# Early projection blocks of a hybrid decoder layer in 1024-column blocks, three of eight steps by seven products

## The chip, the cores and the metric

One core of one Trainium2 chip runs the whole layer in one launch. The metric is the device time of that core in microseconds, the median of several runs.

## The reference

One layer on 256 positions of width 2048 (float32):

```python
a = rmsnorm(h, norm_mix_pre)
proj = a @ w_in                       # 2048 x 17408
q_a, k_a, v_a, q_r, f_r, i_r, g_r, gate_a, gate_r = split_columns(proj)
# attention: 3 groups (window, dilation) x 8 heads of 128, rotary q and k,
#            group outputs mixed by their softmax denominators
# recurrence: S_t = diag(f_t) S_{t-1} + k_t v_t^T, o_t = S_t^T q_t, 8 heads,
#            f = lb + (1 - lb) sigmoid(f_r), k = 1 - f, per-head RMSNorm, gain, times silu(g_r)
y = sigmoid(gate_a) * (attn @ w_attn_branch) + sigmoid(gate_r) * (r_out @ w_hgrn_branch)
h = h + rmsnorm(y @ w_mix_out, norm_mix_post)
a = rmsnorm(h, norm_ffn_pre)
gt, up = split(a @ w_ffn_gate_up)     # 2048 x 11264
h = h + rmsnorm((silu(gt) * up) @ w_ffn_down, norm_ffn_post)
```

The columns of `w_in` are q, k, v (3072 each), the recurrence's q, f, i, g (1024 each) and the two gates (2048 each).

## The kernel before

Every product is made of three matmuls in a rounded format: the kernel splits each float32 operand into a high and a low part, ScalarE writing the high one (a copy), VectorE the low one (a subtraction), and adds high x high, high x low and low x high in PSUM. The weights stream once from memory, through three slots of 8 KB per partition (`raw`), and are split into `w` slots two steps ahead of TensorE (`AHEAD`).

The work is a list of blocks, written out in program order. Each engine takes its instructions in the order in which the Python loop issues them.

- An "N" block makes 512 columns with the activations as the stationary operand: 8 chunks of 12 matmuls. The value blocks take every second position of `xT` for a side (`parity`), for the attention's dilation. A "W" block makes 256 columns with the weights as the stationary operand (4 chunks of 16 matmuls), so that its result comes out transposed.
- A wide block (`Wide`) makes 1024 columns in steps of 256 rows of weights. A whole step has 24 matmuls. A step "by seven" takes seven products of three matmuls for eight, by sums of weight blocks (VectorE, `split_wide`) and of activation blocks (`seven_sums`). Four of the products (p1, p5, p6, p7) have PSUM banks of their own, which `gather` adds up after the last step by seven; the four results, keys (side, group), are added to that by the evacuation. A wide block thus holds all eight banks, and the next one uses the two groups of four (`acc`, `aux`) the other way round. The high and low parts of the raw differences (`dh`, `dl`) have one buffer each.

In the loop over wide steps, step i comes in this order: the split of step i + 2, the loads, the matmuls of step i (`multiply_wide`), `gather` after the last step by seven, one turn of the evacuation that stands first in `evacs`; in the feed-forward also, at step 1, `turn_act`, which transposes on TensorE the product u of gate and up of the block before. At the end of a block its evacuation joins `evacs` and takes its first turn.

Program order before: g (2 N blocks), f and the recurrence's q (W), i (N), then twice, once for each half of the heads, three value blocks (N) and six rotary q and k blocks (W); eight gate blocks (N); eight branch blocks, attention and recurrence in turn; the mix (N); then the feed-forward: a first gate and a first up block (N), ten wide gate/up blocks (`GATE_UP`: eight steps, of which the third, fifth and seventh by seven), and two wide down blocks (`DOWN`: 22 steps, six by seven, with `prep`, which makes the activations' sums).

Beside the blocks run two `lanes` of generators, one turn of each per chunk: the opening (norm, tables), the recurrence of each half (its levels, with work on GpSimd, ScalarE, VectorE and small matmuls), and the attention of each head (15 turns). `flush(lanes...)` before the branch blocks ends what is left of them. Large intermediate tiles (`fslot`) share 15 slots.

Of the kernel before, what the change touches and what calls it, by code (L numbers as in the profile page):

```python
# [2 lines left out]

# [16 lines left out]
P = 128  # L20
# [16 lines left out]
H7 = (0, 1, 2)  # L37
GATE_UP = [(3, 0), (4, 0), (0, 1), (5, 0), (1, 1), (6, 0), (2, 1), (7, 0)]
DOWN = [[(m, m in by7) for m in range(KF // 2)] for by7 in (range(4, 20, 3), range(3, 19, 3))]

N_RAW, N_SPLIT, AHEAD, WARM, BRIDGE = 6, 3, 2, 8, 6


class Block:
# [7 lines left out]
    def __init__(self, kind, w, nk, col, xs, evac, parity=False, pre=None, mid=None, post=None):  # L52
        self.kind, self.w, self.nk, self.col = kind, w, nk, col
        self.xs, self.evac, self.parity = xs, evac, parity
        self.pre, self.mid, self.post = pre, mid, post
        self.per = 4 if kind == "W" else 2
        self.width = 1024 // self.per
        self.steps = nk // self.per
        self.banks = None


class Wide:
# [7 lines left out]
    def __init__(self, w, cols, order, xs, seven, evac, prep=None, pre=None, turn=1):  # L70
        self.w, self.cols, self.order, self.xs, self.seven = w, cols, order, xs, seven
        self.evac, self.prep, self.pre, self.turn = evac, prep, pre, turn
        self.last7 = max(i for i, (m, s) in enumerate(order) if s)
        self.bank, self.open, self.rest = {}, set(), None
# [3 lines left out]
def tile_hybrid_block(ctx: ExitStack, tc: tile.TileContext, t, out):  # L78
# [29 lines left out]
    def p3(s, dtype, n, bufs, tag=None):  # L108
        return act_pool[0].tile([P, n], dtype, tag=tag or s, bufs=bufs, name=nm(s))
# [34 lines left out]
    eps = cpool.tile([P, 2], F32, name="eps")  # L144
# [7 lines left out]
    r1p = cpool.tile([P, 2], F32, name="r1p")  # L152
# [4 lines left out]

    ph1 = ExitStack()
    kp = ph1.enter_context(tc.tile_pool(name="kp", bufs=1, reuse_waits="tile"))
    fp = ph1.enter_context(tc.tile_pool(name="fp", bufs=1, reuse_waits="tile"))  # L160

    act_pool = []

    def fslot(s):
        return fp.tile([P, 1024], F32, tag="f", bufs=15, name=nm(s))

    def ptile(s):
        pool, n = (act_pool[0], 2) if act_pool else (fp, 5)
        return pool.tile([P, 512], F32, tag="p", bufs=n, name=nm(s))

    cs = kp.tile([P, 2, S], F32, name="cs")
# [5 lines left out]
    gainr = kp.tile([P, HW], F32, name="gainr")  # L177
    tabs = kp.tile([P, 4, S], F32, name="tabs")
    lb = kp.tile([P, 8], F32, name="lb")
    lb1 = kp.tile([P, 8], F32, name="lb1")  # L180


    blocks, chunks, pairs = [], [], []
    wides, steps = [], []

    def add(*args, **kw):
        b = Block(*args, **kw)
        blocks.append(b)
        for c in range(b.steps):
            chunks.append([b, c, None, None, None])  # L190

    def add_wide(w, nk, col, xs, ev):
        for i in range(2):
            add("W", w, nk, col + 256 * i, xs, both_halves(ev, i))
# [11 lines left out]
    def parts(j):  # L206

        return (slice(0, 512), slice(512, 1024)) if j == 0 else (slice(0, 1024),)

    def load(j):  # L210
        if j >= len(chunks):
            load_wide(j - len(chunks))
            return
        b, c = chunks[j][:2]
        if j % 2 == 0:
            pairs.append(stream.tile([P, 2048], F32, tag="raw", bufs=N_RAW // 2, name=nm("raw")))
        raw = pairs[j // 2][:, j % 2 * 1024 : j % 2 * 1024 + 1024]
        rows = b.per * P
        src = b.w[c * rows : (c + 1) * rows, b.col : b.col + b.width]
        src = src.rearrange("(k p) c -> p k c", p=P)  # L220
        dst = raw.rearrange("p (k c) -> p k c", k=b.per)
        n = len(parts(j))
        for i in range(n):
            ks = slice(i * b.per // n, (i + 1) * b.per // n)
            nc.sync.dma_start(dst[:, ks, :], src[:, ks, :])
        chunks[j][2] = raw
# [4 lines left out]
    def split(j, only=None):  # L231
        if j >= len(chunks):
            split_wide(j - len(chunks))
            return
        raw = chunks[j][2]
        if chunks[j][3] is None:
            w = wslot()
            chunks[j][3:] = [w[:, :1024], w[:, 1024:]]
        wh, wl = chunks[j][3:]
        for n, k in enumerate(parts(j)):  # L240
            if only in (None, n):
                nc.scalar.activation(wh[:, k], raw[:, k], AF.Copy)  # L242
                nc.vector.tensor_sub(wl[:, k], raw[:, k], wh[:, k].bitcast(F32))  # L243

    def multiply(j, sides=(0, 1)):
# [4 lines left out]
        for s in sides:  # L250
            if s == 1 and c == 0 and b.mid:
                b.mid()
            for kk in range(b.per):
# [3 lines left out]
                if b.kind == "N":  # L257
                    ps = b.banks[s]
                    if b.parity:
                        sh, sl = (  # L260
                            x.rearrange("p (j two) -> p two j", two=2)[:, s, :]
                            for x in (xh, xl)
                        )
                    else:
                        sh, sl = (x[:, s * P : (s + 1) * P] for x in (xh, xl))
# [9 lines left out]
    def add_wide_block(*args, **kw):  # L275
        b = Wide(*args, **kw)
        wides.append(b)
        for i in range(len(b.order)):
            steps.append([b, i, None, None])

    def load_wide(n):
        if n % 2 or n // 2 >= len(steps):
            return
        n //= 2
        b, i = steps[n][:2]
        m = b.order[i][0]
        raw = stream.tile([P, 2048], F32, tag="raw", bufs=N_RAW // 2, name=nm("raw"))
        for g, col in enumerate(b.cols):
# [1151 lines left out]
```

## Time and profile before

| | us |
|---|---|
| median of 3 runs | 1741.58 (1741.17 to 1743.07) |
| span of the profiled execution | 1740.1 |
| PE busy | 1725.0 |
| DVE busy | 1264.3 |
| ACT busy | 886.1 |
| POOL busy | 74.0 |

The profiled execution's span is 1.48 us below the median of the runs. A busy PE is the time in which at least one matmul is on record; matmuls overlap in the array, so that the pitch from one to the next is read from the start times, not from the duration of one. L115 is the helper through which nearly all matmuls go; the tile names tell them apart. L243 and L242 are the split of chunks, L306 and L308 that of whole wide steps, L312 to L326 that of steps by seven, L371 to L375 `gather`, L1161 to L1167 the feed-forward's evacuation, L1127 `turn_act`.

### The profile page before, as it was taken

To read this page: it belongs to the slowest core of one execution; us is meant where nothing else is said; L and a number is where in the kernel's file an instruction comes from. 1 tells how busy PE (TensorE), PEld (TensorE's weight loads), DVE (VectorE), ACT (ScalarE), POOL (GpSimd) and SP (SyncE) were. 2 spreads that over 40 slices of the span, in tenths; PEclk is the share of its full clock that TensorE was granted. 3 is DMA by queue.
4 is the path that set the end of the run, shared out by engine and by line. 5 is a ranking of instruction groups with operands and counts; after the bars stand their busy time and mean duration, and the time that the engine had idled before them with its cause. 6 is when DMAs were issued, how large, how long until landed. Compare 5 with 4: busy or idle time off the path is not lost.

```text
span 1740.1 us, 21588 instructions
## 1 busy us (share of the span) xinstructions
PE 1725.0 (99%) x8424; PEld 1448.6 (83%) x8424; DVE 1264.3 (73%) x1372; ACT 886.1 (51%) x1050; POOL 74.0 (4%) x54
## 2 busy tenths in 40 slices
PE   9999999999999999999999999999999999999997
PEld 7888888888888888888888877888888888888886
DVE  5767647877546776544566577888888888898998
ACT  6545455344444444454444466555555555665663
POOL 0002413400000000000000000000000000000000
PEclk9999999999999999999999999999999999999999
DMA  7655445455454554455555745655555555666553
GB/s 271 202 192 194 145 150 165 146 160 186 163 170 161 185 188 169 170 169 193 193 179 185 266 168 175 214 199 201 205 194 194 194 194 199 221 209 218 195 197 116
DMA packets 201222, 325.91 MB, mean 187 GB/s; under 512 B 10096, under 2 KB 76832, under 8 KB 201120
## 3 DMA queue, kind: packets, MB, share of 16 engines
q1 hardware_dynamic: 198848, 319.41, 54.4%
q10 hardware_dynamic: 2272, 5.12, 0.8%
q8 instruction: 66, 1.08, 0.2%
q14 instruction: 36, 0.29, 0.1%
HBM read 322.40 MB, written 2.10 MB: 186 GB/s over the span
## 4 chain that ended last, share of the span: by engine, by line
PE 95%; DVE 2%; ACT 1%; issue 1%; DMA 0%; POOL 0%; DVEq 0%; ACTq 0%
PE acc L115 71%; PE aux L115 22%; DVE w L243 1%; ACT w L242 1%; DVE w L677 0%; PE aux L453 0%; PE aux L724 0%; DMA gpost<-in_norm_mix_post 0%; PE acc L1127 0%; DVE fz L1256 0%; PE aux L1127 0%; DVE x L776 0%; PE aux L440 0%; ACT junk L1210 0%; POOL x L770 0%
## 5 line engine op out<-in xcount | busy, mean ns | idle before, releaser
L243 DVE TENSOR_TENSOR w<-raw,w 128x1024 fp32r<-128x1024 f32 (+1 forms) x353 | 444.4, 1260 | 365.5 <-ACT w L242 362.7
L242 ACT ACTIVATE w<-raw 128x1024 fp32r<-128x1024 f32 (+1 forms) x353 | 372.9, 1057 | 481.1 <-PE acc L115 470.7
L115 PE MATMUL acc<-w,xT 128*128 128x512 f32 x1728 | 409.1, 395 | 0.0
L115 PEld LDWEIGHTS acc<-w,xT 128*128 128x128 f32 x1728 | 326.3, 191 | 65.8
L115 PE MATMUL acc<-xT,w 128*128 128x256 f32 (+1 forms) x2048 | 362.6, 338 | 0.0
L115 PEld LDWEIGHTS acc<-xT,w 128*128 128x128 f32 x2048 | 313.0, 189 | 45.1
L308 DVE TENSOR_TENSOR wl<-raw,w 128x2048 fp32r<-128x2048 f32 x82 | 187.5, 2287 | 34.0 <-ACT w L306 33.9
L306 ACT ACTIVATE w<-raw 128x2048 fp32r<-128x2048 f32 x82 | 156.6, 1910 | 81.7 <-PE aux L115 32.1
L115 PE MATMUL acc<-w,hT 128*128 128x512 f32 x622 | 182.5, 392 | 1.5 <-DVE w L243 1.2
L115 PEld LDWEIGHTS acc<-w,hT 128*128 128x128 f32 x622 | 115.8, 188 | 26.9 <-DVE w L243 2.5
L115 PE MATMUL aux<-w,hT 128*128 128x512 f32 x430 | 135.7, 389 | 0.0
L324 DVE TENSOR_TENSOR wl<-sum,w 128x2048 fp32r<-128x2048 f32 x42 | 96.2, 2290 | 33.8 <-ACT w L320 32.7
L317 ACT ACTIVATE w<-sum 128x1024 fp32r<-128x1024 f32 x42 | 44.7, 1063 | 111.0 <-DVE sum L312 106.7
L115 PEld LDWEIGHTS aux<-w,hT 128*128 128x128 f32 x430 | 80.7, 188 | 16.7
L115 PE MATMUL acc<-w,yT 128*128 128x512 f32 x384 | 88.0, 390 | 0.3 <-DVE w L243 0.3
L115 PEld LDWEIGHTS acc<-w,yT 128*128 128x128 f32 x384 | 71.8, 188 | 15.5 <-DVE w L243 0.7
L115 PE MATMUL acc<-w,a 128*128 128x512 f32 x268 | 83.7, 389 | 0.0
L115 PE MATMUL aux<-w,a 128*128 128x512 f32 x268 | 83.7, 389 | 0.0
L115 PE MATMUL aux<-wl,hT 128*128 128x512 f32 x215 | 83.7, 389 | 0.0
L115 PE MATMUL acc<-wl,hT 128*128 128x512 f32 x215 | 83.7, 389 | 0.0
L326 DVE TENSOR_TENSOR dl<-raw,dh 128x1536 fp32r<-128x1536 f32 x42 | 73.5, 1751 | 0.0
L323 ACT ACTIVATE dh<-raw 128x1536 fp32r<-128x1536 f32 x42 | 61.9, 1474 | 0.0
(263 smaller groups left out, 2015.3 us busy)
## 6 DMA issues: line engine op xcount, KB each, us to landing
raw<-in_w_in SPq DMA_DIRECT2D x271, 512.0 KB, 4.5
raw<-in_w_ffn_gate_up SPq DMA_DIRECT2D x176, 512.0 KB, 4.4
raw<-in_w_ffn_down SPq DMA_DIRECT2D x88, 512.0 KB, 4.8
raw<-in_w_mix_out SPq DMA_DIRECT2D x32, 512.0 KB, 4.9
raw<-in_w_attn_branch SPq DMA_DIRECT2D x16, 512.0 KB, 4.5
raw<-in_w_hgrn_branch SPq DMA_DIRECT2D x16, 512.0 KB, 4.6
hx<-in_x ACTq DMA_DIRECT2D x4, 512.0 KB, 9.9
x<-in_x SPq DMA_DIRECT2D x3, 512.0 KB, 10.0
```

What stands on the lines that cost most here:

```text
L115: nc.tensor.matmul(ps, lhsT, rhs, start=start, stop=stop, skip_group_check=True)
L242: nc.scalar.activation(wh[:, k], raw[:, k], AF.Copy)
L243: nc.vector.tensor_sub(wl[:, k], raw[:, k], wh[:, k].bitcast(F32))
L306: nc.scalar.activation(hi, raw, AF.Copy)
L308: nc.vector.tensor_sub(lo, raw, hi.bitcast(F32))
L317: nc.scalar.activation(hi[:, :1024], s[:, :1024], AF.Copy)
L323: nc.scalar.activation(dhi, d, AF.Copy)
L324: nc.vector.tensor_sub(lo, s, hi.bitcast(F32))
L326: nc.vector.tensor_sub(dlo, d, dhi.bitcast(F32))
```

## The change

- The gates of the attention branch, half of those of the recurrence branch, the values, g and i become eight wide blocks of 1024 columns (`early`) at the start of the kernel. The first (`PLAIN`) has no steps by seven, the other seven have `GATE_UP`. The sums of `xT` (`pair_sums`) are made during the first. The remaining two gate blocks stay N blocks, behind the q and k blocks.
- Gates and values are put in DRAM (`stored`, issued from ScalarE's queue, one store per 128 x 512 tile) and fetched (SyncE's queue) before they are used: the values at the last k block of each half, the gates behind all q and k blocks. The values are fetched with the rows' parity apart, so the strided weights of the value blocks go.
- In a step by seven of a block without `prep`, the products from the sums (`by_sums`) go before those from the raw differences (`by_raw`, of which p1 is the last). That holds for the early blocks and for the feed-forward's ten gate/up blocks; the down blocks keep their order.
- Lanes advance twice in a wide step (`between`). A recurrence level has one turn more between its last elementwise product and its matmuls. The heads go into one `queue`, and a lane that is empty takes the next.
- All four recurrence-branch blocks go before the four attention-branch blocks. `turns` advance twice per chunk.
- `fslot` has 16 slots. The early blocks have a pool of their own (`p0`), closed during the first f block; two small tiles are padded, so that the pools behind them start at other addresses.

The core of the diff:

```diff
+    def totals(b, then):
+        while "r1c" not in ready:
+            yield
+        for n, key in enumerate(((0, 0), (0, 1), (1, 0), (1, 1))):
+            src = b.bank[key]
+            if b.rest:
+                nc.vector.tensor_add(b.rest[key], src, b.rest[key])
+                src = b.rest[key]
+            then(key, src)
+            if n % 2:
+                yield
+    def stored(names, func):
+        def ev(b):
+            def then(key, src):
+                s, g = key
+                e = b.rest[key] if b.rest else eslot()
+                nc.scalar.activation(e, src, func, scale=r1c[:, s : s + 1])
...
+                nc.scalar.dma_start(waits[names[g]][s * P : (s + 1) * P, :], e)
+            return totals(b, then)
+        return ev
+    def evac_g(b):
+        def then(key, src):
...
+            sig = ptile("sig")
+            nc.scalar.activation(sig, src, AF.Sigmoid, scale=r1c[:, s : s + 1])
+            nc.vector.scalar_tensor_tensor(
+                out=sig, in0=src, scalar=r1c[:, s : s + 1], in1=sig, op0=OP.mult, op1=OP.mult
+            )
+            nc.vector.tensor_mul(gN[g][:, s, :], sig, gainr[:, g * 512 : (g + 1) * 512])
+        return totals(b, then)
...
-        prod((0, 1), act_of(0, 1), d, 2)
-        prod((0, 0), sums(3), d, 0)
-        prod("p1", act_of(0, 0), d, 1, last)
-        prod("p6", sums(1), t, 2, last)
-        prod("p5", sums(0), t, 1, last)
-        prod("p7", sums(2), t, 0, last)
-        prod((1, 1), act_of(1, 1), t, 3)
+        def by_raw():
+            prod((0, 1), act_of(0, 1), d, 2)
+            prod((0, 0), sums(3), d, 0)
+            prod("p1", act_of(0, 0), d, 1, last)
+        def by_sums():
+            prod("p6", sums(1), t, 2, last)
+            prod("p5", sums(0), t, 1, last)
+            prod("p7", sums(2), t, 0, last)
+            prod((1, 1), act_of(1, 1), t, 3)
+        for part in (by_raw, by_sums) if b.prep else (by_sums, by_raw):
+            part()
+            if part is by_raw or not b.prep:
+                between()
+                between = lambda: None
...
             nc.gpsimd.tensor_mul(xv[:, :, right], xv[:, :, right], qv[:, :, right])
             yield
+            yield
             ps = aux()
...
+    early = [
+        (("a", 0), ("a", 1), COL_GA, 512),
+        (("a", 2), ("a", 3), COL_GA + 1024, 512),
+        (("r", 0), ("r", 1), COL_GB, 512),
+    ]
+    early += [(("v", g, 0), ("v", g, 1), COL_V + 1024 * g, 512) for g in range(3)]
+    early += [("g", "g", COL_GR, 512), ("i", "i", COL_IR, 512)]
+    for n, (k0, k1, col, step) in enumerate(early):
+        ev = {"i": evac_i, "g": evac_g}.get(k0) or stored(
+            (k0, k1), AF.Copy if k0[0] == "v" else AF.Sigmoid
+        )
+        add_wide_block(w_in, (col, col + step), GATE_UP if n else PLAIN, xT,
+                       lambda m: x7[m], ev, n % 2 == 0, mid=more_x if n == 0 else None, halves=n == 0)
```

More of the change, by code (lines that the diff above doesn't have):

```diff
@@ L204, in both_halves, with add_wide_block @@
         return go
[L206 to L212, printed above, removed]
-            return
[L214 to L226, printed above, removed]
+    def add_wide_block(*args, **kw):
+        b = Wide(*args, **kw)
+        wides.append(b)
+        for i in range(len(b.order)):
+            n = len(steps)
+            slots.append(lambda n=n: load_wide(n))
+            items.append((steps, n, len(slots) - 1))
+            steps.append([b, i, None, None])
@@ L501, in flush, with advance_lanes, flush_lanes @@
             advance(q)
+    def advance_lanes():
+        for lane in lanes:
+            if not lane and queue:
+                lane.append(queue.popleft())
+            advance(lane)
+    def flush_lanes():
+        while queue or any(lanes):
+            advance_lanes()
     xt = [hslot("x") for _ in range(4)]
@@ L653, in nslot, with fetch, fetch_values @@
     def nslot(s):
         return fslot(s).rearrange("p (b c) -> p b c", b=2)
[L656 to L662 removed]
+    def fetch(dst, key, rows, **sizes):
+        nc.sync.dma_start(dst, waits[key].rearrange(rows, **sizes))
+    def fetch_values(half):
+        for g in range(3):
+            vN[half, g] = nslot("v")
+            fetch(vN[half, g], ("v", g, half), "(j two) c -> j two c", two=2)
@@ L778, in level @@
             yield
+            yield
             ps = aux()
```

430 lines of the change are left out of this document (227 added, 203 removed).

## The prediction

> **What bounds the kernel now.** I read the page first, for the engine that fills the span; then the chain of waits, for what one matmul costs in each stage; then the timelines of one feed-forward block, engine by engine, for the spare time around the matmuls.
>
> ```profile
> span 1740.1 us, 21588 instructions
> ...
> PE 1725.0 (99%) x8424; PEld 1448.6 (83%) x8424; DVE 1264.3 (73%) x1372; ACT 886.1 (51%) x1050; POOL 74.0 (4%) x54
> ...
> PE 95%; DVE 2%; ACT 1%; issue 1%; DMA 0%; POOL 0%; DVEq 0%; ACTq 0%
> ...
> raw<-in_w_in SPq DMA_DIRECT2D x271, 512.0 KB, 4.5
> ```
>
> TensorE is never out of work and carries 95% of the chain. So the time changes by matmul time taken out, plus every new wait of TensorE.
>
> ```profile
> 497.01 11.20 PE acc L115 x48
> ...
> 661.78 10.93 PE acc L115 x48
> ...
> 1159.68 10.88 PE aux L115 x48
> ...
> 1202.05 10.88 PE acc L115 x48
> ...
> 1244.59 10.88 PE aux L115 x48
> ...
> 1286.96 10.88 PE acc L115 x48
> ...
> 1414.08 10.88 PE aux L115 x48
> ```
>
> The chain's columns are start, time, what. Durations of single matmuls overlap; the pitch is these times over 48: 233.3 ns in the value blocks (every second column of xT as weights), 227.7 ns in the gate blocks, 226.7 ns in the wide blocks. A whole step (24 matmuls) is 5.44 us, a step by seven (21) 4.76 us. The last five rows each open a feed-forward block at its step 0; I call that instant T.
>
> **What the change takes out.** Sixteen 512-column blocks (gates a, half of gates r, values, g, i) become eight wide ones, one whole and seven with three steps by seven: 16 x 96 = 1536 matmuls become 192 + 7 x 183 = 1473. 63 x 0.2267 = 14.3 us. The 576 matmuls of the values lose the strided weights: 576 x 6.6 ns = 3.8 us. The other 960 go from 227.7 to 226.7 ns: 1.0 us. Together **-19.1 us**, all on the path. Everything else of TensorE (f, qr, q, k, branches, mix, FFN) has as many matmuls as before.
>
> **What the new order inside a step by seven adds in the feed-forward.** Where a block has no `prep`, `by_sums` now goes before `by_raw`, so p1 is the last product of the step, not the third of seven. The ten gate/up blocks have no `prep` either. `gather` starts with p1.
>
> ```profile
> 1408.13 0.68 DVE L372 TENSOR_TENSOR e<-aux,e 128x512 f32<-128x512 f32 x1
> 1410.92 2.28 DVE L308 TENSOR_TENSOR wl<-raw,w 128x2048 fp32r<-128x2048 f32 x1
> 1413.12 2.48 DVE L1161 TENSOR_TENSOR e<-acc,e 128x512 f32<-128x512 f32 x4
> 1415.51 1.21 DVE L312 TENSOR_TENSOR sum<-raw 128x1024 f32<-128x1024 f32 x1
> 1416.76 0.69 DVE L318 TENSOR_TENSOR sum<-raw,sum 128x512 f32<-128x512 f32 x1
> ...
> 1419.30 2.29 DVE L324 TENSOR_TENSOR wl<-sum,w 128x2048 fp32r<-128x2048 f32 x1 [1.13 <-ACT w L320]
> 1421.51 1.75 DVE L326 TENSOR_TENSOR dl<-raw,dh 128x1536 fp32r<-128x1536 f32 x1
> 1423.18 1.41 DVE L1167 SCALAR_TENSOR_TENSOR e<-e,r2c,e 128x512 f32<-128x512 f32 x2
> ```
>
> ```profile
> 1405.96 0.60 ACT L371 ACTIVATE e<-aux 128x512 f32<-128x512 f32 x1
> 1408.68 1.92 ACT L306 ACTIVATE w<-raw 128x2048 fp32r<-128x2048 f32 x1 [2.12 <-PE acc L115]
> 1413.84 0.73 ACT L1164 ACTIVATE e<-e,r2c 128x512 f32<-128x512 f32 x1 [3.23 <-DVE e L1161]
> 1418.21 1.06 ACT L320 ACTIVATE w<-sum 128x1024 fp32r<-128x1024 f32 x1 [0.31 <-DVE sum L319]
> 1420.55 1.90 ACT L306 ACTIVATE w<-raw 128x2048 fp32r<-128x2048 f32 x1
> ```
>
> With T = 1414.08, step 6 ends at T-5.44. Before, p1 is copied (L371) at T-8.12 and the first add (L372) runs at T-5.95. With p1 last the copy starts at T-5.40 and ends at T-4.80: the add at T-4.75, 1.20 us later. From there DVE has no slack until L1167: split, four adds, sums, two lows, then the two multiplies that make u (the 1.13 us idle before L324 is ScalarE's answer to those same sums). So u comes 1.20 us later, and TensorE's next work after step 1 (T+10.88) is the transpose of u, in order.
>
> How much room is there? One block of the trace answers:
>
> ```profile
> 1203.83 1.22 DVE L312 TENSOR_TENSOR sum<-raw 128x1024 f32<-128x1024 f32 x1
> ```
>
> Here the sums start at T+1.78 (T = 1202.05), not T+1.43: 0.35 us late. From the chain, that block lasts 1244.59 - 1202.05 = 42.54, its neighbours 42.37 (1159.68 to 1202.05; 1244.59 to 1286.96). 0.35 us late cost 0.17, so the room is 0.18 us, and 1.20 us late costs 1.02. Nine blocks transpose a u made so: **+9.2 us**. Bounds: 0 (something absorbs it) and 9 x 1.2 = 10.8.
>
> **What the early blocks' evacuation adds.** They have the same step order, and the evacuation comes in two turns: keys (0,0), (0,1) at the block's end, (1,0), (1,1) after the next block's step 0, on DVE behind the split of step 2. New here: each key's tile is stored to DRAM from ScalarE's queue.
>
> ```profile
> 956.63 0.90 ACTq L985 DMA_DIRECT2D gpost<-in_norm_mix_post  x2
> 957.56 3.34 ACTq L991 DMA_DIRECT2D hx<-in_x  x4
> 960.95 0.60 ACT L1002 ACTIVATE junk<-acc 128x512 f32<-128x512 f32 x1 [3.26 <-issue]
> ```
>
> ```profile
> 1.23 0.93 SPq L225 DMA_DIRECT2D raw<-in_w_in  x2
> ```
>
> ScalarE waits while it issues. An issue took 0.45 (gpost), 0.47 (SP's 256 KB pieces, the shape of a store) or 0.84 us (hx). I take 0.47, and 0.1 for the store's wait on its own tile. On the clock of T: first add 0.24 (as above), sums at 1.5; ScalarE is held by two functions of 0.72 and two issues to 3.5; its halves to 5.6; lows 7.9 and 9.55; adds 10.2 and 10.8; function, store, function, store: 12.8. Only now comes step 3's split: ScalarE 14.7, DVE 17.0. TensorE is there at 10.88 + 4.76 = 15.64 and waits 1.4. Step 4's sums start at 17.0, its low ends 6.1 later (as L312 to the end of L324), TensorE is there at 22.45: 0.6 more. 2.0 us at each of the five ends of stored blocks with products by seven: **+10.0 us** (no issue cost: 0.3 each, 1.5; at 0.84: 3.5 each, 17.5). Block 0 has no adds and no gather: 0, covered by some 2 us of room.
>
> Block g is worse: add, sigmoid on ScalarE, multiply, multiply, in DVE's order, so DVE stands through each sigmoid.
>
> ```profile
> 58.81 0.69 ACT L644 ACTIVATE sig<-acc,r1c 128x512 f32<-128x512 f32 x1
> ```
>
> ```profile
> 61.62 0.75 DVE L646 SCALAR_TENSOR_TENSOR sig<-acc,r1c,sig 128x512 f32<-128x512 f32 x1
> 62.40 0.69 DVE L649 TENSOR_TENSOR g<-sig,gainr 128x512 f32<-128x512 f32 x1
> ```
>
> A key takes 2.85 us, a turn 5.7. Sums of step 2 at 5.95, low at 12.0 (TensorE there at 10.88: 1.1); second turn 13.6 to 19.3, its last sigmoid at 17.9, then step 3's split 19.8 and 22.05 (TensorE there at 16.8: 5.3); step 4 0.6. **+7.0 us**; bounds 1 (DVE catches up) and 9.
>
> **What moves.** Both recurrences now run under the q/k blocks with their rotary evacuation; before, the first ran under i and v.
>
> ```profile
> 145.00:277.00 132.00, 131.64 (x653) 111.41 (x652) 82.12 (x82) 65.99 (x94) 32.88 (x19) 0.99 0.47 160
> ...
> 285.00:332.00 47.00, 45.32 (x288) 40.26 (x287) 44.33 (x40) 19.65 (x28) 25.00 (x12) 0.96 0.42 135
> ```
>
> ```profile
> 304.64 1.97 PE L115 MATMUL aux<-x 128*128 128x64 f32 x16 [1.45 <-DVE x L776]
> ...
> 321.40 1.97 PE L115 MATMUL aux<-x 128*128 128x64 f32 x16 [0.23 <-DVE x L776]
> ...
> 332.41 11.41 PE L115 MATMUL acc<-xT,w 128*128 128x512 f32 x64
> ```
>
> ```profile
> 295.43 4.15 DVE L677 TENSOR_TENSOR w<-sum,tabs 64x512 f32<-64x512 f32 x2
> ...
> 329.86 1.38 DVE L677 TENSOR_TENSOR w<-sum,tabs 64x512 f32<-64x512 f32 x2
> ```
>
> Columns: span; busy of PE, PEld, DVE, ACT, POOL; granted clock; DMA. Under q/k, DVE is busy 44.33 of 47 us (L677 takes 4.15 us beside POOL, 1.38 without); TensorE loses 1.68 idle (1.45 + 0.23 for late x) and 4% of clock, 1.9: 3.6 us. Under i and v it loses 0.36 + 1% of 132: 1.7. Two under q/k, with the added turn covering the idle 1.68 of each: 3.8 against 5.3 now, **-1.5 us**. Bounds: no loss left (-5.3), and each losing double (+9.1).
>
> Costed at nothing: 24 stores and 12 fetches, beside a DMA share of 0.4 to 0.5; the fetches stand on SP ahead of weights, whose three slots hold six W chunks (2.85 us each, 11.41 for four) against 4.5 us to land, so a fetch that waits two chunks for its slot is covered. The second half's attention has 32 turns in two lanes under gate and recurrence-branch chunks (32); what is left, the last two splits, is wanted three chunks later. Startup loads the same bytes for its first product.
>
> Sum: -19.1 + 9.2 + 10.0 + 7.0 - 1.5 = **+5.6 us** on the span of 1740.1. The median of the runs is 1741.58, 1.48 above that span; I add the sum to it: 1747.
>
> **Rivals.** (1) Faster: the early blocks' waits are not there, since a store issue does not hold ScalarE and DVE catches up before step 3. For: DVE's work in such a block is 3 x 6.6 (1.21 + 2 x 0.69 + 2.29 + 1.75) + 5 x 2.29 + 8 adds of 0.62 = 36 of 41.5 us (183 x 0.2267). Against: L1002's 3.26. -19.1 - 1.5 + 9.2 = -11.4: 1730. It decides once the early waits sum to under 7.9 of the 17.0 (then faster by over 3.5). (2) Only the feed-forward wait is absorbed: 5.6 - 9.2 = -3.6: 1738. Against it stands the 42.54. (3) A store issue costs 0.84, as hx: +7.5: 1755. (4) DVE and POOL pace the q/k blocks at the upper bound: +10.6: 1758. (5) TensorE's 5.3 us stop after g lowers the clock: the 285 to 332 window shows 0.96 around a 1.45 us stop, 1.9 us; it would give 1749. The Trainium skill ("TensorE: Matmul & The Clock Gate", Part 1) puts half clock after an idle window of about 3.4 us; by it, an estimate, 1.7 us more.
>
> **How the numbers follow.** Forecast 0.42, (1) 0.25, (2) 0.12, (3) 0.09, (4) 0.06, (5) 0.06. A change of under 0.2% (3.5 us) can't be told from none: 1738.1 and 1745.1 are the borders. Faster: (1) and 0.08 of (2), 0.33. Same: the rest of (2) and 0.13 of the forecast's lower end, 0.17. Slower 0.50. The forecast's own range is 1741 to 1752; 8 in 10 needs (1) and (3): 1728 to 1756.
>
> **What would show it.** Before each transpose of u, TensorE idle about 1 us, released by DVE; feed-forward blocks of 43.4 us. In each early block after the second, a stop before step 3, the longest after g. Matmuls down by 63, value pitch at 226.7. Wrong if the gate/up blocks stay at 42.4, or early wide blocks last 41.5 us each.

## The result: 1763.5 us, slower

The changed kernel takes 1763.49 us (median; 1761.73 to 1764.46), 21.9 us more than the 1741.55 us of the kernel before beside it: ratio 1.0124, 95% interval 1.0110 to 1.0138. The direction was the forecast's, the size was not: 1763 lies above the range's upper end, 1756.

The page of the changed kernel, span, busy times and the chain's shares by engine:

```profile
span 1762.7 us, 21573 instructions
...
PE 1719.0 (98%) x8356; PEld 1432.1 (81%) x8357; DVE 1390.0 (79%) x1466; ACT 917.3 (52%) x1052; POOL 77.2 (4%) x54
...
PE 70%; DVE 16%; issue 6%; ACT 5%; DMA 2%; ACTq 0%; POOL 0%; SPq 0%; DVEq 0%; POOLq 0%
```

Line numbers are now the changed kernel's: L119 is the helper that was L115. TensorE's share of the chain falls from 95% to 70%, VectorE's rises from 2% to 16%. Outside its busy time TensorE spends 1762.7 - 1719.0 = 43.7 us instead of 15.1: 28.6 us more idle. Its busy time falls by 6.0 us, not by the 19.1 of the forecast; part of the difference is clock, as the next views show. TensorE's waits, by who ended them (us in total, times, longest):

```profile
PE acc L119 <- DVE w L295: 6.4, 6, 2.0
PE acc L119 <- ACT xT L524: 3.8, 1, 3.8
PE aux L119 <- DVE wl L342: 3.6, 3, 1.8
PE aux L1218 <- DVE e L1258: 2.7, 10, 0.3
PE acc L119 <- DVE wl L342: 2.5, 3, 1.0
...
PE aux L119 <- DVE x L884: 2.1, 2, 1.1
```

L295 is mostly the split of the q and k chunks, L524 the copies of the transposed input, L342 the low half of a whole wide step's split (L340 the high one), L1258 the feed-forward's u, L884 a recurrence level's product. Two of these stand nowhere in the forecast's sum: L295 and L524. (L358 and L360, in later views, are the low halves of a step by seven.) The table of stages shows the same (columns: span; busy of PE, PEld, DVE, ACT, POOL; granted clock; DMA), the start, the other early blocks, q and k with the recurrences; the last row is the start of the kernel before:

```profile
6.00:70.00 64.00, 58.33 (x258) 46.16 (x256) 44.93 (x76) 39.66 (x65) 0.00 (x0) 0.95 0.70 247
70.00:375.00 305.00, 293.89 (x1273) 238.64 (x1272) 248.54 (x200) 157.35 (x131) 0.95 (x1) 0.99 0.63 211
470.00:660.00 190.00, 182.58 (x1132) 160.44 (x1131) 173.69 (x182) 88.07 (x140) 65.88 (x33) 0.99 0.48 157
```

```profile
6.00:70.00 64.00, 63.77 (x316) 52.38 (x314) 44.08 (x68) 41.65 (x68) 0.00 (x0) 1.00 0.76 262
```

TensorE idles 5.7 us in the start, 11.1 in the early blocks and 7.4 under q and k. The start of the kernel before loses 0.2.

### The profile page after: what moved, and what is told of

Same layout as the page of the kernel before. It is cut to its first block, busy times and chain, and to the rows that moved or that the text cites. A ratio compares the mean times of both kernels' runs of the same rounds, so it can differ in the third digit from the quotient of the medians.

```text
span 1762.7 us, 21573 instructions
## 1 busy us (share of the span) xinstructions
PE 1719.0 (98%) x8356; PEld 1432.1 (81%) x8357; DVE 1390.0 (79%) x1466; ACT 917.3 (52%) x1052; POOL 77.2 (4%) x54
## 4 chain that ended last, share of the span: by engine, by line
PE 70%; DVE 16%; issue 6%; ACT 5%; DMA 2%; ACTq 0%; POOL 0%; SPq 0%; DVEq 0%; POOLq 0%
PE acc L119 47%; PE aux L119 21%; DMA raw<-in_w_in 2%; DVE wl L358 2%; DVE wl L342 2%; DVE dl L360 2%; DVE w L295 2%; ACT w L354 1%; DVE e L1252 1%; DVE sum L346 1%; ACT w L340 1%; DVE sum L353 1%; DVE sum L352 1%; ACT e L726 1%; DVE e L1258 1%
## 5 line engine op out<-in xcount | busy, mean ns | idle before, releaser
L295 DVE TENSOR_TENSOR w<-raw,w 128x1024 fp32r<-128x1024 f32 x224 | 284.9, 1274 | 173.7 <-ACT w L294 172.8
L119 PE MATMUL acc<-xT,w 128*128 128x256 f32 (+1 forms) x2048 | 369.6, 340 | 5.2 <-DVE w L295 5.2
L294 ACT ACTIVATE w<-raw 128x1024 fp32r<-128x1024 f32 x224 | 236.3, 1057 | 255.6 <-PE acc L119 236.9
L119 PEld LDWEIGHTS acc<-xT,w 128*128 128x128 f32 x2048 | 312.4, 189 | 51.3 <-DVE w L295 7.4
L342 DVE TENSOR_TENSOR wl<-raw,w 128x2048 fp32r<-128x2048 f32 (+1 forms) x131 | 283.9, 2173 | 64.5 <-ACT w L340 61.6
L340 ACT ACTIVATE w<-raw 128x2048 fp32r<-128x2048 f32 (+1 forms) x131 | 237.3, 1817 | 71.0 <-issue 22.3
L358 DVE TENSOR_TENSOR wl<-sum,w 128x2048 fp32r<-128x2048 f32 x63 | 144.4, 2291 | 59.0 <-ACT w L354 57.7
L119 PE MATMUL acc<-w,hT 128*128 128x512 f32 x622 | 184.8, 391 | 1.5 <-DVE w L295 1.2
L119 PE MATMUL acc<-w,xT 128*128 128x512 f32 x578 | 172.4, 396 | 5.7 <-ACT xT L524 3.8
L119 PE MATMUL aux<-w,hT 128*128 128x512 f32 x430 | 138.0, 389 | 0.0
L119 PEld LDWEIGHTS acc<-w,hT 128*128 128x128 f32 x622 | 115.8, 188 | 27.0 <-DVE w L295 2.5
L119 PEld LDWEIGHTS acc<-w,xT 128*128 128x128 f32 x578 | 108.8, 190 | 29.7 <-ACT xT L524 4.2
L119 PE MATMUL aux<-w,xT 128*128 128x512 f32 x344 | 112.3, 395 | 1.6 <-ACT w L340 1.6
L360 DVE TENSOR_TENSOR dl<-raw,dh 128x1536 fp32r<-128x1536 f32 x63 | 110.3, 1752 | 0.0
L357 ACT ACTIVATE dh<-raw 128x1536 fp32r<-128x1536 f32 x63 | 93.2, 1480 | 4.7 <-PE aux L119 2.1
L119 PEld LDWEIGHTS aux<-w,hT 128*128 128x128 f32 x430 | 80.7, 188 | 16.7
L119 PE MATMUL acc<-w,yT 128*128 128x512 f32 x384 | 88.2, 390 | 0.0
L119 PE MATMUL acc<-w,a 128*128 128x512 f32 x268 | 83.8, 389 | 1.7 <-DVE e L1252 1.7
L119 PEld LDWEIGHTS acc<-w,yT 128*128 128x128 f32 x384 | 71.8, 188 | 15.2 <-DVE w L295 0.4
L119 PE MATMUL aux<-w,a 128*128 128x512 f32 x268 | 83.7, 389 | 0.0
L119 PE MATMUL aux<-wl,hT 128*128 128x512 f32 x215 | 83.6, 389 | 0.0
```

The costliest lines, as they stand in the source:

```text
L119: nc.tensor.matmul(ps, lhsT, rhs, start=start, stop=stop, skip_group_check=True)
L294: nc.scalar.activation(wh, raw, AF.Copy)
L295: nc.vector.tensor_sub(wl, raw, wh.bitcast(F32))
L340: nc.scalar.activation(hi[:, c], raw[:, c], AF.Copy)
L342: nc.vector.tensor_sub(lo[:, c], raw[:, c], hi[:, c].bitcast(F32))
L357: nc.scalar.activation(dhi, d, AF.Copy)
```

## The losses of the changed kernel, place by place

**The feed-forward.** Its blocks in the chain of the changed kernel (start, time, what: the first wide block's step 0, the four adds of each block's evacuation, the first down block):

```profile
1086.56 10.88 PE aux L119 x48
...
1129.16 2.48 DVE e L1252 x4
...
1476.11 2.48 DVE e L1252 x4
...
1520.93 22.05 PE acc L119 x96
```

Eight blocks take 1476.11 - 1129.16 = 346.95, 43.37 each, against 42.37 before. The first wide block starts 11.6 us later than before (1074.93), the first down block 22.1 us later (1498.83): these blocks add 10.5, and the places ahead of them 11.6 in spite of the matmul time saved.

**The start.** TensorE, timeline:

```profile
15.05 0.60 PE L517 MATMUL aux<-ident,x 128*128 128x128 f32 x4
...
18.03 0.39 PE L119 MATMUL acc<-w,xT 128*128 128x512 f32 x1
22.20 0.79 PE L119 MATMUL acc<-w,xT 128*128 128x512 f32 x1 [3.78 <-ACT xT L524]
...
27.86 0.60 PE L517 MATMUL aux<-ident,x 128*128 128x128 f32 x4
```

ScalarE in the same stretch:

```profile
19.45 1.06 ACT L340 ACTIVATE w<-raw 128x1024 fp32r<-128x1024 f32 x1 [1.86 <-DMA raw<-in_w_in]
20.73 1.06 ACT L340 ACTIVATE w<-raw 128x1024 fp32r<-128x1024 f32 x1 [0.23 <-DMA raw<-in_w_in]
21.69 0.82 ACT L524 ACTIVATE xT<-aux,colg 128x256 fp32r<-128x256 f32 x2
```

The input's transposes for step 2 are done on TensorE at 15.7. Their copies stand in ScalarE's order behind the split of step 3, and that split waits for its weights (1.86 <-DMA). So step 2, whose own operands are long in place, waits for step 3's load. After the 3.78 us stop TensorE runs slowly: 22.20 to 27.86 for 12 matmuls, 0.47 us each, instead of 0.2267. The stop and the slow stretch come to 27.86 - 18.26 - 12 x 0.2267 = 6.9 us. Two more waits, of 0.74 and 1.07 us, stand before steps 6 and 7, for xT again. In all, the first wide block takes 56.6 us from its first product to the next block's, and 47.4 in experiment two, where these waits are gone: 9.2 us lost.

**The ends of the stored blocks.** The chain at one of them:

```profile
155.74 1.75 DVE dl L360
157.48 0.61 DVE e L712
...
158.12 0.73 ACT e L726
...
158.88 0.33 ACTq L729
...
159.25 0.73 ACT e L726
...
160.00 0.33 ACTq L729
...
160.43 1.93 ACT w L340
...
162.38 0.07 DVE wl L342
```

It is the forecast's order: gather's late work, add, function, store issue, function, store issue, and only then step 3's split. TensorE takes up step 3 at 164.73 after 0.81 us idle. A store's issue holds ScalarE for 0.33 us, not 0.47. The five stops before step 3 are 0.63 to 0.99 us. By their first products, the five blocks behind stored ends last 43.01 to 43.33 us, where 183 matmuls at 0.2267 take 41.48: 8.7 us lost in all.

The trace of before had this price, in a row that the forecast did not use: ScalarE's stores of the output, four in the trace, take 0.34 to 0.36 us each to issue (shortest, median and longest in ns). The forecast took its 0.47 from a load.

```profile
L1259 ACTq DMA_DIRECT2D out_dram<-fz x4: 338/344/358, 1727.0 to 1735.8; - x4
```

**After g.** TensorE's stops, with the end of the slow stretch:

```profile
331.81 0.39 PE L119 MATMUL acc<-w,so 128*128 128x512 f32 x1
333.48 0.50 PE L119 MATMUL acc<-wl,so 128*128 128x512 f32 x1 [1.27 <-DVE wl L358]
...
335.74 0.50 PE L119 MATMUL acc<-w,so 128*128 128x512 f32 x1 [0.84 <-DVE e L712]
...
341.17 0.49 PE L119 MATMUL aux<-w,xT 128*128 128x512 f32 x1 [1.58 <-ACT w L340]
343.49 0.79 PE L119 MATMUL aux<-wl,xT 128*128 128x512 f32 x1 [1.83 <-DVE wl L342]
...
348.71 0.39 PE L119 MATMUL aux<-wl,xT 128*128 128x512 f32 x1
```

VectorE in the second of g's two turns, ahead of step 3's split:

```profile
335.01 0.68 DVE L712 TENSOR_TENSOR e<-acc,e 128x512 f32<-128x512 f32 x1
336.48 0.75 DVE L748 SCALAR_TENSOR_TENSOR sig<-e,r1c,sig 128x512 f32<-128x512 f32 x1 [0.79 <-ACT sig L747]
337.26 0.69 DVE L751 TENSOR_TENSOR g<-sig,gainr 128x512 f32<-128x512 f32 x1
```

Each key holds VectorE for 2.86 us (the next one's add comes at 337.87), 0.79 of it idle behind ScalarE's sigmoid, as in the forecast (2.85). From 331.81 to 348.71 there are 34 matmuls: 16.90 - 34 x 0.2267 = 9.2 us lost, 5.5 of them the four stops. The rest is mostly a slow pitch: 12 matmuls from 343.49 to 348.71, 0.435 us each.

**Under q and k.** L786, the rotary products on VectorE, from 470 to 520 us (shortest, median and longest in ns), in the changed kernel and in one in which a single GpSimd instruction has gone to VectorE:

```profile
L786 DVE TENSOR_TENSOR w<-sum,tabs x6: 684/1182/2312, 478.5 to 515.0; 64x512 f32<-64x512 f32 x6
```

```profile
L786 DVE TENSOR_TENSOR w<-sum,tabs x6: 684/686/687, 479.5 to 508.2; 64x512 f32<-64x512 f32 x6
```

The same instruction takes up to 3.4 times as long beside GpSimd's work. In the changed kernel its three pairs (at 478.5, 494.7 and 512.7 us) all overlap a GpSimd operation.

## The experiments

Each experiment is the changed kernel with one or more edits, unless said otherwise; a ratio is to the kernel before, in the same runs. "Gain" is the median's distance from 1763.5.

**One: the feed-forward's order undone.**

```diff
-for part in (by_raw, by_sums) if b.prep else (by_sums, by_raw):
+for part in (by_raw, by_sums) if b.prep or b.turn else (by_sums, by_raw):
```

`turn` is set for the feed-forward's gate/up blocks and not for the early blocks.

> The changed kernel, but with the feed-forward's gate/up blocks back in the old order inside a step by seven (raw differences first, p1 third). My theory: p1 last delays gather by 1.2 us and stops TensorE about 1.0 us before each of nine transposes of u; blocks go from 43.36 back to 42.37 us: 9 to 10.5 us less, about 1754. Rival (the order costs nothing, the blocks are longer for another reason, such as the tiles' new addresses or the DMA): within 2 us of 1763.5.

1755.8 us, ratio 1.0083 (1.0069 to 1.0096), gain 7.7. The chain's first and last wide block:

```profile
1091.09 10.88 PE aux L119 x48
...
1472.62 10.88 PE acc L119 x48
```

Nine blocks in 381.53, 42.39 each: the loss of 1.0 us a block is p1's place, shown. The gain of 7.7 is under the 9 to 10.5 of the blocks. The trace shows where the rest went: the first wide block starts 4.5 us later than in the changed kernel, though nothing ahead of it was edited. From 470 to 670 us TensorE's granted clock is at half in four stretches of 3.4 us, and in the changed kernel in one. Three more cost some 5.1 us (see "The clock" below).

**Two: the first product's copies a step earlier.**

```diff
-        if 0 < c < KD // 2 - 1:
-            transpose_in(xt, colg, xT, c + 1)
+        if c + 2 < KD // 2:
+            transpose_in(xt, colg, xT, c + 2)
```

> The changed kernel, but each pair of x blocks is transposed one step sooner in block 0 (two steps ahead, not one). Theory: at step 2 TensorE waits 3.8 us for xT, whose copy stands on ScalarE behind a split that waits for its weights' DMA, and then runs at a lower clock for some 2.5 us, and it waits 1.8 us for xT again before steps 6 and 7; with the copies one step ahead all this goes: 6 to 8 us less, about 1756. Rival (startup is bound by the bytes that must land, in whatever order): TensorE waits the same time for the weights instead, 0 to 2 us less.

1754.95, ratio 1.0080 (1.0067 to 1.0093), gain 8.5. The copies now run at 15.95, 5.7 us earlier, ahead of the split that waits for its load (at 19.11):

```profile
15.95 0.82 ACT L524 ACTIVATE xT<-aux,colg 128x256 fp32r<-128x256 f32 x2
```

TensorE is busy 64.00 of the 64 us from 6 to 70, at full clock. So the start's loss was order on ScalarE, not bytes. The gain goes past the 6 to 8 us that were expected.

**Three: the stores issued from GpSimd's queue.**

```diff
-                nc.scalar.dma_start(waits[names[g]][s * P : (s + 1) * P, :], e)
+                nc.gpsimd.dma_start(waits[names[g]][s * P : (s + 1) * P, :], e)
```

> The changed kernel, but the 24 stores of gates and values are issued from GpSimd's queue instead of ScalarE's. Theory: at five block ends ScalarE's issues (0.33 to 0.47 us each, four per block) push step 3's split past TensorE's arrival; without them the wait before step 3 falls from about 1.2 us to 0 to 0.3 and that before step 4 stays at about 0.4: 4 to 6 us less, about 1758.5. Rival (VectorE alone is late): the waits stay, 0 to 1 us less.

1759.96, ratio 1.0107 (1.0091 to 1.0122), gain 3.5, slightly under what was expected. All five stops before step 3 are gone: of the waits for L342 one of 1.8 us is left, g's. Two issues of 0.33 us are thus enough to decide whether step 3's split is in time, but the next experiment removes the same stops with the issues still on ScalarE, earlier in its order.

**Four: the stored blocks' evacuation in one turn.** All four keys at the block's end, ahead of step 2's split.

```diff
-            if n % 2:
+            if n % 2 and not (b.rest and then.__name__ == "then_stored"):
                 yield
```

> The changed kernel, but the evacuation of the six stored blocks takes one turn instead of two: four adds, four functions, four stores at the block's end. Theory: ScalarE's issues then lie ahead of the split of step 2, where there is room, and step 3's split no longer waits for them: the waits before steps 3 and 4 (7.2 us over five blocks) go, as they did with the stores on another queue: 3 to 6 us less, about 1759. Rival (the issues hold ScalarE wherever they stand): the wait moves to step 2, 0 us less.

1758.54, ratio 1.0086 (1.0074 to 1.0098), gain 5.0. The five stops are gone here too, and the five blocks take 41.48 us each, all of the 8.7 us. So what costs is the second turn's place between two splits, and the issue only adds to it. The median shows less than the blocks, since the clock was lower in these runs.

**Five: g's evacuation spread.** Four adds and four sigmoids in the first turn, then one key's two multiplies in each of four turns, so that VectorE does not stand behind a sigmoid.

```diff
+        for key in keys:
+            nc.vector.tensor_add(b.rest[key], b.bank[key], b.rest[key])
+            nc.scalar.activation(gN[g][:, s, :], b.rest[key], AF.Sigmoid, scale=r1c[:, s : s + 1])
+        for key in keys:
+            yield
...
```

> The changed kernel, but g's evacuation does its four adds and four sigmoids in the first turn and then one key's two multiplies in each of four turns, so VectorE never stands through a sigmoid. Theory: the four stops after g (1.3, 0.8, 1.6 and 1.8 us idle, some 8 us with the lowered clock) fall to under 1.5 us in all: 5 to 8 us less, about 1757. Rival (VectorE has too much work there in any order): the stops move to the next steps, 0 to 2 us less.

1760.47, ratio 1.0105 (1.0092 to 1.0118), gain 3.0. The four stops after g are gone, but two new ones for L358 (0.47 and 1.66 us) come later in the block behind: part of VectorE's backlog is moved, not removed. That block lasts 44.7 us instead of 50.7, so g's place gains 6.0, within the 5 to 8 that were expected of the run; the median gains only 3.0, and the trace has two half-clock stretches more under q and k.

**Six: all eight early blocks whole**, 63 matmuls more, without sums, gather or adds.

```diff
-        add_wide_block(w_in, (col, col + step), GATE_UP if n else PLAIN, xT,
+        add_wide_block(w_in, (col, col + step), PLAIN, xT,
```

> The changed kernel, but all eight early wide blocks are whole: no steps by seven in them, so no gather and no adds in their evacuation (the sums of x are still made and not used); 63 matmuls more. Theory: the 14.3 us of matmuls that the products by seven save are given back by waits that they bring (7.2 us after the five stored blocks, 8 us after g with its lower clock), so this run is within 3 us of the changed kernel, 1761 to 1765. Rival (those waits belong to the evacuation and the stores, not to the steps by seven): 1770 or more.

1760.83, ratio 1.0109 (1.0095 to 1.0123), 2.7 faster than with the products by seven. From 70 to 375 us TensorE waits for nothing. So in the changed kernel the early blocks lost to VectorE all of the 14.3 us that the 63 matmuls saved, and a little more.

**Seven: one subtraction of each recurrence level on VectorE instead of GpSimd.**

```diff
-            nc.gpsimd.tensor_sub(xv, bv, bv[:, :, w - 1 : w].to_broadcast([P, n, 2 * w]))
+            nc.vector.tensor_sub(xv, bv, bv[:, :, w - 1 : w].to_broadcast([P, n, 2 * w]))
```

> The changed kernel, but the first subtraction of each recurrence level (128x1024, 12 in all, 2.5 us each on GpSimd) is done by VectorE. Theory: under the q and k blocks VectorE is late because its two-input operations stand while GpSimd reads (L677 took 4.15 us beside GpSimd, 1.38 alone); with less GpSimd work TensorE's losses in the two recurrences (some 5 us each) fall by 2 to 6 us in all, about 1759.5, though VectorE has 12 operations of 1.2 us more. Rival (VectorE is simply full): 4 us more or worse.

1757.77, ratio 1.0091 (1.0078 to 1.0104), gain 5.7. The stage of q and k:

```profile
470.00:660.00 190.00, 188.82 (x1173) 167.81 (x1173) 170.72 (x201) 89.80 (x142) 36.40 (x24) 0.98 0.50 164
```

VectorE has 19 instructions more in this window, 12 of them the subtractions (1.22 us each), and is busy for less time than before the edit, 170.7 us against 173.7, while TensorE's idle time falls from 7.4 to 1.2 us. VectorE was not too full: it was slowed. The Trainium skill ("SBUF — State Buffer", "Who interferes with whom") says that a VectorE operation with two SBUF inputs and a GpSimd operation that reads SBUF block each other for a whole instruction. The rows agree in kind: L786, with two SBUF inputs, takes 0.68 us or up to 2.3.

**Eight: the kernel before, with value blocks that take consecutive positions.** This leaves out the parity of the rows: the values belong to other positions than the reference's.

```diff
-scaled(vN, (half, g), r1p, nslot), parity=True)
+scaled(vN, (half, g), r1p, nslot))
```

> The kernel before, with the value blocks taking consecutive positions as weights instead of every second one (the values then belong to other positions; nothing else differs). Theory: the pitch of the 576 value matmuls falls from 233.3 to 227.7 ns: 3 to 4 us less, about 1738. Rival (the pitch of these blocks has another cause, the tiles' addresses or the lanes beside them): within 1 us of 1741.5.

1736.23, ratio 0.9969 (0.9957 to 0.9981): 5.4 us faster, with an interval of about 3.3 to 7.5. The value blocks' steps go from 11.20 to

```profile
439.88 10.93 PE acc L115 x48
```

which is 576 x 5.6 ns = 3.2 us. The forecast's term of 3.8 (which counted 226.7) is borne out by the pitch. The median's 5.4 is more than the pitch gives; the clock is part of it (0.998 in the median run, 0.996 in the kernel before).

**Nine: five edits together**, those of experiments one, two, four, five and seven.

> The changed kernel with five edits at once: raw products first in the feed-forward's steps by seven, the first product's copies made a step earlier, stored blocks evacuated in one turn, g's multiplies spread over turns, the levels' first subtraction on VectorE. Theory (five separate losses): alone they gave 7.7 + 8.5 + 5.0 + 3.0 + 5.7 = 29.9, so 1763.5 - 29.9 = 1734, within 4 us; that is 7 to 8 below the kernel before. Rival (one wait hides behind another, so what one edit frees the next wait takes): no better than 1742, the kernel before.

1725.4 us, ratio 0.9902 (0.9889 to 0.9916): 38.1 us faster than the changed kernel and 15.8 faster than the kernel before. This is the version that beats both. Its page, and its stages of the early blocks and of q and k:

```profile
span 1723.5 us, 21597 instructions
...
PE 1706.3 (99%) x8356; PEld 1431.9 (83%) x8357; DVE 1378.1 (80%) x1478; ACT 913.8 (53%) x1052; POOL 44.5 (3%) x42
```

```profile
70.00:375.00 305.00, 302.81 (x1366) 250.30 (x1365) 257.92 (x216) 164.96 (x144) 0.95 (x1) 1.00 0.65 221
470.00:660.00 190.00, 188.82 (x1189) 168.17 (x1189) 167.26 (x204) 88.85 (x144) 34.58 (x23) 0.98 0.49 160
```

With the waits gone, TensorE's busy time is 1706.3, 18.7 below the 1725.0 of the kernel before: the 19.1 us of matmul time in the forecast is there. Neither theory holds on the medians: the edits gave more than their sum of 29.9. The part on the clock, below, says why.

**Ten: the same, with raw products first in the early blocks too.**

```diff
-for part in (by_raw, by_sums) if b.prep or b.turn else (by_sums, by_raw):
+for part in (by_raw, by_sums):
```

> As the kernel with the five edits, but raw products first in the early blocks' steps by seven too, so p1 is the third product there and the gather can start 1.2 us earlier. Theory (in the early blocks VectorE is late by the whole chain of adds, so 1.2 us earlier is 1.2 us less wait where a wait is left: after g, two waits of about 2 us in sum): 1 to 2.5 us faster than the five edits alone. Rival (raw first makes the raw differences' low halves, which VectorE writes last, the first wanted; the steps then wait for them): slower than the five edits alone by 2 us or more.

1726.85, ratio 0.9913 (0.9899 to 0.9926). The two intervals overlap, so neither order is shown to be faster, and neither theory is borne out. The waits differ in kind, though:

```profile
PE aux L119 <- DVE dl L360: 4.4, 4, 2.1
```

Raw first makes TensorE wait for dl, which VectorE writes last (the rival's mechanism, below its price); sums first waits 1.9 us for wl. In the early blocks nothing is seen to be won by moving p1. In the feed-forward there was 1 us a block.

**Eleven: the kernel before, with experiment seven's edit.**

> The kernel before with one edit: the recurrence levels' first subtraction on VectorE instead of GpSimd. Theory A (the loss beside GpSimd lies in every recurrence that runs under q and k, so the kernel before loses it once, the changed one twice): about half of the 5.7 us that the changed kernel gained, 2 to 4 us faster. Theory B (the order of work of the change makes the loss, the kernel before hides it): within 1 us of the kernel before.

1737.09, ratio 0.9978 (0.9968 to 0.9987): 4.1 us faster. So this loss is in the kernel before too. Its two stages of the recurrence, which stand in the prediction, become:

```profile
145.00:277.00 132.00, 132.00 (x656) 112.08 (x655) 81.74 (x87) 67.20 (x96) 18.53 (x13) 0.99 0.49 160
285.00:332.00 47.00, 46.97 (x300) 42.14 (x299) 43.26 (x47) 19.02 (x28) 12.36 (x7) 0.96 0.44 138
```

TensorE's idle time goes from 0.36 and 1.68 us to 0 and 0.03, 2.0 of the 4.1 us; the runs' clock is also about 0.001 higher, which is worth 2. The clock of the second stage stays at 0.96 though the stop is gone, so a stop is not needed to lower it. The forecast's rival (5) had read this row as if it were. In this run that stage has one stretch at half clock, from 328.5 to 331.9 us, behind matmuls that have no gap between them (TensorE's timeline, then the stretch with its clock of 0.50):

```profile
324.06 1.97 PE L115 MATMUL aux<-x 128*128 128x64 f32 x16
325.86 1.90 PE L115 MATMUL aux<-ones,x 128*128 128x1 f32 x16
```

```profile
328.50:331.80 3.30, 3.30 (x13) 2.82 (x12) 3.09 (x5) 0.00 (x0) 0.00 (x0) 0.50 0.69 205
```

**Twelve: the five edits with whole early blocks** (g's evacuation as in the change).

> The five edits' kernel with all eight early blocks whole (63 matmuls more; g's evacuation as it was in the change, since whole blocks have no adds). It prices the products by seven in a kernel whose other waits are gone. Theory (a matmul costs its pitch): 63 x 0.2267 = 14.3 us less what g still waits, about 2: 11 to 14 us slower than the five edits. Rival (the early blocks by seven still lose to VectorE what they save): within 4 us of the five edits.

1736.07, ratio 0.9966 (0.9952 to 0.9980): 10.7 us slower than experiment nine, just under the 11 to 14 expected. The products by seven, worth less than nothing in experiment six, are worth most of their 14.3 us once VectorE's order around them is mended.

**Thirteen and fourteen: the five edits in two groups**, the early blocks' two (experiments four and five) and the other three.

> The changed kernel with the two edits of the early blocks' evacuation: stored blocks in one turn, g's multiplies spread over turns. Alone they gave 5.0 and 3.0. Theory (they help one another: g spread alone left a backlog of 1.66 and 0.47 us in the blocks after it, which the one turn clears): 10 to 16 us faster than the changed kernel. Rival (they only add): 8.0, so 6 to 10.

> The changed kernel with the other three: raw products first in the feed-forward, the first copies a step earlier, the levels' subtraction on VectorE. Alone 7.7 + 8.5 + 5.7 = 21.9. Theory (the excess is in the early pair): 20 to 24 us faster than the changed kernel. Rival (the excess is here, where the feed-forward edit alone gave 7.7 although its nine blocks measured 1.0 each and the last one 1.5): 26 to 32.

The early two: 1751.7, ratio 1.0055 (1.0043 to 1.0068), gain 11.8 against 8.0 for the sum of each alone. The other three: 1739.91, ratio 0.9983 (0.9975 to 0.9992), gain 23.6 against 21.9. The groups sum to 35.4.

**The clock.** Experiment nine's 38.1 is 8.2 more than the five gains, but the runs differ in clock. Experiment four's six runs alone go from 1752.07 us at a mean granted clock of 0.996 to 1760.51 at 0.991: 8.4 us, where 0.005 of 1758 is 8.8. Taking (1 - clock) times its span off each run gives its time at full clock. The clocks are given to 0.001, so this is good to a us or two:

| experiment | gain of the median | at full clock | half-clock windows in the trace |
|---|---|---|---|
| one | 7.7 | 9.5 | 8 |
| two | 8.5 | 5.0 | 2 |
| four | 5.0 | 9.5 | 7 |
| five | 3.0 | 3.0 | 4 |
| seven | 5.7 | 8.3 | 6 |
| sum of these | 29.9 | 35.3 | |
| thirteen (four, five) | 11.8 | 12.7 | 4 |
| fourteen (one, two, seven) | 23.6 | 22.5 | 3 |
| nine (all) | 38.1 | 34.5 | 2 |

Such a window is 3.41 us at half clock, some 1.7 us lost; the changed kernel's trace has five, the end of the kernel left out. At full clock the five edits add up, alone, in groups and together, so no edit is seen to help another: the excess of 8 is clock. (The column leaves out something real where an edit removes a stop, as two and five do: the slow matmuls behind it.)

What sets the clock can be read from the traces, though no run tests it. In all 16 it is either whole or half, and changes only on a grid of 3.41 us. I count the result columns of the matmuls that TensorE starts in each such window, from 10 us on; at the pitch of 0.2267 us it would be 7,700. All 51 windows with under 2,058 were followed by half clock, and none of the 8,020 with over 3,076; of the 47 between, 20 were. A stop lowers the count, and so do the small matmuls of a recurrence, with 64 columns or 1 each, even while TensorE is never idle. If the count is the cause, a run's place on the grid decides whether a short stretch of small matmuls fills a window, and the spread between runs of one kernel would come from there.

## Why the prediction was wrong

On the span, the forecast was +5.6 and the result +22.6. Its terms, with what the traces show in each place:

| term | forecast | found | from |
|---|---|---|---|
| matmul time | -19.1 | -18.7 | busy time, experiment nine |
| feed-forward blocks | +9.2 | +10.5 | first wide block to first down block; 1.0 a block |
| stored ends | +10.0 | +8.7 | lengths of five blocks |
| after g | +7.0 | +9.2 | start times, 331.81 to 348.71 us |
| recurrences | -1.5 | about +4 | idle 7.4 and 1% of clock against 5.3 before |
| start | 0 | +9.2 | length of the first block |

The found terms sum to +22.9. The changed kernel's first product also starts 1.5 us earlier (6.79 us, 8.27 before), which the forecast did not count. The recurrences' figure is the roughest.

- **The step that failed most** is the last sentence of "What moves": "Startup loads the same bytes for its first product." The bytes are the same, the order on ScalarE is not. A whole step is two loads of 512 KB; the split of step 3 waits for its load, and the copies that step 2 needs are issued behind it. Experiment two gives 8.5 us of it back. The forecast costed the start by its resource (bytes) and not by its queue; it followed the queue behind a late instruction in the later early blocks and not here.
- **The second** is the recurrences' term, -1.5, wrong in sign. It took the level's added turn to cover TensorE's wait for x (L776 then, L884 now). Those waits remain, 2.1 us, and a larger one, 5.2 us for the chunks' split (L295), stands beside them. The forecast's own row showed the cause, L677 at 4.15 us beside GpSimd and 1.38 without; it priced the waits that this had made so far and not the slowing itself under two recurrences. Rival (4), "DVE and POOL pace the q/k blocks", had the mechanism; its +10.6 was too much. Experiment seven shows that all but 1.2 us of these waits go when one GpSimd instruction a level does, and eleven that the kernel before loses to it too.
- **The feed-forward** was right in mechanism and size. 43.4 us a block was forecast and 43.37 found, and experiment one restores 42.39. TensorE stops twice before each transpose of u, for 0.2 and 0.3 us, and with the refills that comes to 1.0. The last block, where TensorE waits 1.7 us for the adds (L1252), adds the rest.
- **The early blocks** came out close in sum (17.0 and 17.9), in part by luck: the errors in the terms go opposite ways. The path is the forecast's. The stored ends cost 8.7 instead of 10.0: an issue holds ScalarE for 0.33 us and not 0.47, and the stops before step 3 are 0.63 to 0.99 and not 1.4. After g it is 9.2 instead of 7.0: the stops themselves are 5.5, 1.5 under the forecast, and 3.7 go to the slow clock and the refills. That is what rival (5) said, which put 1.9 on it. The Trainium skill's page that this rival named ("TensorE: Matmul & The Clock Gate", Part 1) puts half clock after an idle window of about 3.4 us. The traces agree in the two speeds, half and whole, and in the window's length, and not in the idleness, and the measurement decides: in the start the clock is at half from 20.95 to 27.78 us, though TensorE had been idle for only 2.5 us by then, and behind g from 341.80 to 348.63, with four matmuls started in the 3.41 us ahead of it. It stays whole after the 1.65 us stop in experiment nine's early blocks.
- **Rival (1)**, no early waits, fell. VectorE is idle for 56 of the 305 us of the early blocks, about the room that this rival counted on, and TensorE waits for it all the same, since the work comes in an order in which the room can't be used.

What stays open: whether the count of columns is what lowers the clock, since no run varies it alone, and why the runs of some single edits had more half-clock stretches under q and k than the changed kernel.

## What to carry to other kernels

Before costing a moved block at nothing, follow what each engine's queue has directly ahead of the first operand it needs; an instruction that waits for a DMA holds all that is issued behind it, however early that is ready. Products saved on TensorE are worth their time only if the engine that prepares and gathers them does so in an order that fits: here the same 63 matmuls were worth -2.7 us, and 10.7 after four small changes of order and one of engine. Before gains of a few us are added or compared, look at the granted clock of each run: here it moved one kernel's time by 8 us. Where a row of one operation shows two durations, find its neighbour on the other engine first; that one move gained 4.1 us in the kernel before as well, 2.0 of it as idle time.

## What was not expected of the hardware

- A VectorE operation of 0.68 us took up to 2.3 us beside GpSimd, and giving VectorE 12 more operations of 1.22 us made its busy time in the stage 3 us shorter.
- One stop of 3.78 us cost 6.9: 12 matmuls behind it took 0.47 us each instead of 0.2267. The clock was at half for 6.83 us, here and behind g.
- The clock also fell to half behind small matmuls without a gap: in experiment eleven from 328.5 to 331.9 us, after a window of 3.41 us with 2,512 result columns.
- A DMA issue of a 128 x 512 tile on ScalarE's queue took 0.33 us. Stores of the output took 0.34 to 0.36 in the trace of before, where loads on the same queue took 0.35 to 0.95.
